# Dilated attention: the score matmuls of two heads issued in turn, in the two row halves of TensorE and two PSUM banks

## The chip, the cores and the metric

The kernel runs on one core of one Trainium2 chip. The metric is the device time of one execution in microseconds; before the change it is 2756.3 us, the median of 3 runs (2753.86 to 2757.47).

In the views of the profile PE is TensorE (its matmuls), PEld its weight loads, DVE is VectorE, ACT is ScalarE, POOL is GpSimd and SP the engine that issues most transfers. L1087 is line 1087 of the kernel.

## What is computed

The reference is a two-layer encoder over 768 tokens, 512 of one sequence and 256 of another. Each layer has a mixer of four branches (a convolution module, spatial gating, latent attention, dilated attention), joined by sigmoid gates, and a convolutional feed-forward part. The change touches one step of the dilated attention. It has three groups (window, dilation) of four heads of 64 dimensions; a group's scores are the products of each query with the keys at multiples of the dilation inside its window:

```
DIL_GROUPS = ((128, 1), (512, 4), (2048, 16))
for g, (win, dil) in enumerate(DIL_GROUPS):
    n_side = (win // 2) // dil
    idx = pos[:, None] + (dil * jnp.arange(-n_side, n_side + 1))[None, :]
    ...
    s = jnp.einsum('bqhd,bqjhd->bhqj', qi[:, :, g], kg, preferred_element_type=jnp.float32)
    s = jnp.where(valid[None, None], s, NEG_INF)
    lse = jax.nn.logsumexp(s, axis=-1)
    p = jnp.exp(s - lse[..., None])
    outs.append(jnp.einsum('bhqj,bqjhd->bqhd', p.astype(vg.dtype), vg))
```

The groups' outputs are then weighted by a softmax over their lse and projected.

## The kernel before

All instructions are unrolled and written out in one order by Python. The large matrices are multiplied as split products: an operand is cut into a high and a low part in the fp32r type, and three matmuls stand for one (`tm`, `fm`; L522 and L498). They are TensorE's main work. Beside them run generators: `go_fast` and `go` put a generator into a list, and `q`, called after each block of split matmuls, moves a planned clock on and lets the generators that are due issue their next instructions. So the small steps of the attention are sprinkled between the matmuls of the projection that runs as the main work. The planned clock sets an order only; on the chip each engine takes its instructions in that order.

For each layer, `mixer` projects dilation group 0, then starts `dil_attn(0)` as a generator and projects group 1, and so on; the attention of group 2 runs beside the projection of the spatial gating. In `dil_proj` the results are normalised and rotated (`dil_norm`), and PE transposes them into `qT` and `kT` (the tile `q`, read by L1029 on ACT and L1030 on DVE). A feature block of 128 partitions, `qT[y]`, holds two heads: head 2y in partitions 0 to 63 and head 2y+1 in 64 to 127. The tokens of groups 1 and 2 are taken with a stride, so there the projection's weight operand is a strided slice of the normalised input.

`dil_attn` makes jobs, two for each block of queries: `par` 0 does the lower heads of both feature blocks, `par` 1 the upper ones. In group 0 a block is one tile of 128 queries with 192 or 256 keys; in groups 1 and 2 it is two tiles with 128 keys each. `pipe` runs the jobs as a pipeline of seven stages: in step i it issues `score` of job i, then `done` of job i-3; a third of a step later `low` of job i and `turn` of job i-1; another third later `expo` of job i, `copy` of job i-1 and `value` of job i-2. The planned step is 2.7 us for group 0 and 4.0 us for the others.

- `score` (L1087, PE): 2 or 4 matmuls of 64 rows in float32, into a PSUM tile `sc` of its own.
- `low` (L1092, L1094, DVE): adds the mask out of `sc` into `P` and takes the minimum of each row.
- `expo` (L1101, ACT): the exponentials.
- `turn` (PE transposes, L511), `copy` (L1121 or L1123, DVE), `value` (L1135 or L1138, PE), `done` (L1144, ACT, and the store to DRAM).

PSUM has eight banks. The mixer's pool keeps two double banks for the projections (`mm`) and four single ones (`ps`), which `sc`, the transposes `pt`, the values `po` and the projection's `q` share. A bank that has been read comes back to the end of the list of free ones.

The score matmuls of one job all lie in the same half of the array's rows: 0 to 63 for `par` 0, 64 to 127 for `par` 1. A job's matmuls stand between split matmuls of 128 rows.

Of the kernel before, what the change touches and what calls it, by code (L numbers as in the profile page):

```python
# [247 lines left out]
class Net:  # L248
# [814 lines left out]
    def dil_job(self, g, si, t0, n, i0, nt, par, qT, kT, v, vs, sh):  # L1063
        nc = self.nc
        if g == 0:
            lo, hi = max(0, 128 * i0 - 64), min(128 * n, 128 * i0 + 192)
            mk = self.h("m0")[:, lo - 128 * i0 + 64:hi - 128 * i0 + 64]
            W = hi - lo
            z = 128 * i0 + 64 - lo
            blocks = ((0, z, vs[si][i0][0:z]), (z, W, vs[si][i0 + 1][0:W - z]))  # L1070
            ts = ((t0 + i0, 128 * t0 + lo),)
        else:
            mk = self.h("m0")[:, 64:192] if (g, si) == (1, 0) else self.h(f"m{g}" + "sp"[si])
            W = 128
            ts = tuple((t, 128 * t) for t in (t0 + i0, t0 + i0 + 1))
        rr = slice(64 * par, 64 * par + 64)
        e = {}

        def score():
            if par == 0:  # L1080
                sh["ot"] = ot = self.pm.tile([128, nt, 264], F32, tag="ot", name=self.nm("ot"), bufs=3)
                sh["ol"] = ot[:, :, 256:260].rearrange("p t (h q) -> p t h q", q=2)
                sh["om"] = ot[:, :, 260:264].rearrange("p t (h q) -> p t h q", q=2)
            e["sc"] = sc = self.ps([128, nt, 2, 256 // nt])
            for x, (t, k0) in enumerate(ts):
                for y in range(2):
                    nc.tensor.matmul(sc[:, x, y, 0:W], qT[y][rr, 128 * t:128 * t + 128], kT[y][rr, k0:k0 + W],  # L1087
                                     start=True, stop=True)

        def low():  # L1090
            e["P"] = P = self.s(nt * 2 * W).rearrange("p (a w) -> p a w", a=nt * 2)
            nc.vector.tensor_add(P, e.pop("sc")[:, :, :, 0:W].rearrange("p t h w -> p (t h) w"),  # L1092
                                 mk.unsqueeze(1).broadcast_to([128, nt * 2, W]))
            nc.vector.tensor_reduce(sh["om"][:, :, :, par], P.rearrange("p (t h) w -> p t h w", t=nt), axis=AX.X,  # L1094
                                    op=ALU.min)

        def expo():
            P = e["P"]
            for x in range(nt):
                for y in range(2):  # L1100
                    nc.scalar.activation(P[:, 2 * x + y, :], P[:, 2 * x + y, :], AF.Exp,  # L1101
                                         bias=sh["om"][:, x, y, par:par + 1], scale=-1.0,
                                         accum_out=sh["ol"][:, x, y, par:par + 1])

        def turn():
            P = e.pop("P")
            e["pt"] = pt = self.ps([128, 4, 128])
            if g == 0:
                for y in range(2):
                    for z, (a, c, _) in enumerate(blocks):  # L1110
                        self.tr(pt[0:c - a, 2 * z + y, :], P[:, y, a:c])
            else:
                for y in range(4):
                    self.tr(pt[:, y, :], P[:, y, :])

        def copy():
            pt = e.pop("pt")
            e["PT"] = PT = self.s().rearrange("p (a q) -> p a q", a=4)
            if W == 192:
                for z, (a, c, _) in enumerate(blocks):  # L1120
                    nc.vector.tensor_copy(PT[0:c - a, 2 * z:2 * z + 2, :], pt[0:c - a, 2 * z:2 * z + 2, :])  # L1121
            else:
                nc.vector.tensor_copy(PT, pt)  # L1123

        def value():
            PT = e.pop("PT")
            if par == 0:
                sh["po"] = self.ps([128, nt, 4, 64])
            po = sh["po"]
            for x, (t, _) in enumerate(ts):  # L1130
                for y in range(2):
                    hc = slice(64 * (2 * y + par), 64 * (2 * y + par) + 64)
                    if g == 0:
                        for z, (a, c, vv) in enumerate(blocks):
                            nc.tensor.matmul(po[:, 0, 2 * y + par, :], PT[0:c - a, 2 * z + y, :], vv[:, hc], start=(z == 0),  # L1135
                                             stop=(z == 1))
                    else:
                        nc.tensor.matmul(po[:, x, 2 * y + par, :], PT[:, 2 * x + y, :], v[t // 3][:, t % 3, hc], start=True,  # L1138
                                         stop=True)

        def done():
            if par == 1:
                ot = sh["ot"]
                nc.scalar.copy(ot[:, :, 0:256].rearrange("p t (h d) -> p t h d", d=64), sh["po"])  # L1144
                self.go_fast(self.dil_store(g, [t for t, _ in ts], ot), 1.0)
                sh.clear()

        return score, low, expo, turn, copy, value, done

    def dil_store(self, g, ts, ot):  # L1150
# [626 lines left out]
```

## Time and profile before

| | |
|---|---|
| median of 3 runs | 2756.3 us |
| the profiled execution, its own time | 2762.6 us |
| its span, first to last instruction | 2760.8 us |
| mean granted TensorE clock | 0.987 |
| TensorE busy (matmuls) | 2709.3 us, 98% |
| weight loads busy | 2461.6 us, 89% |
| VectorE busy | 1731.8 us, 63% |
| ScalarE busy | 1142.6 us, 41% |
| DMA | 258.87 MB, mean 94 GB/s |

Shares are averages over stages with different limits. Matmuls are pipelined and the ends in the rows are modelled, so starts say more than durations; the weight loads run beside the matmuls. The granted clock is given as a share of TensorE's upper level.

### The profile page before, as it was taken

To read this page: it belongs to the slowest core of one execution; us is meant where nothing else is said; L and a number is where in the kernel's file an instruction comes from. 1 tells how busy PE (TensorE), PEld (TensorE's weight loads), DVE (VectorE), ACT (ScalarE), POOL (GpSimd) and SP (SyncE) were. 2 spreads that over 40 slices of the span, in tenths; PEclk is the share of its full clock that TensorE was granted. 3 is DMA by queue.
4 is the path that set the end of the run, shared out by engine and by line. 5 is a ranking of instruction groups with operands and counts; after the bars stand their busy time and mean duration, and the time that the engine had idled before them with its cause. 6 is when DMAs were issued, how large, how long until landed. Compare 5 with 4: busy or idle time off the path is not lost.

```text
span 2760.8 us, 40139 instructions
## 1 busy us (share of the span) xinstructions
PE 2709.3 (98%) x15196; PEld 2461.6 (89%) x15196; DVE 1731.8 (63%) x3048; ACT 1142.6 (41%) x2333; POOL 631.8 (23%) x592
## 2 busy tenths in 40 slices
PE   9999999999999899999999999999999989999999
PEld 8778998888898899999987789888888988999998
DVE  6644347787437966686746443477874378666875
ACT  6443334223224554554544433342232245544553
POOL 3402123112222212222315021221221222122221
PEclk9999999999999999999999999999999999999999
DMA  5101013221233366646721010132212324566566
GB/s 165 43 28 37 30 61 100 71 65 58 62 131 83 95 146 138 148 123 146 190 93 43 28 39 32 58 113 62 62 61 65 127 80 112 144 130 153 130 135 164
DMA packets 143264, 258.87 MB, mean 94 GB/s; under 512 B 20192, under 2 KB 36192, under 8 KB 143072
## 3 DMA queue, kind: packets, MB, share of 16 engines
q1 hardware_dynamic: 118368, 197.59, 22.6%
q0 software_dynamic: 24704, 58.73, 12.3%
q8 instruction: 119, 1.95, 0.3%
q14 instruction: 73, 0.60, 0.1%
HBM read 205.78 MB, written 48.91 MB: 92 GB/s over the span
## 4 chain that ended last, share of the span: by engine, by line
PE 87%; DVE 8%; issue 2%; ACT 2%; POOL 1%; DMA 1%; SPq 0%; DVEq 0%; ACTq 0%; POOLq 0%
PE mm L498 34%; PE ps L498 27%; PE mm L522 16%; PE ps L511 3%; PE ps L1087 2%; DVE wlo L453 2%; PE ps L904 1%; PE ps L1135 1%; PE ps L937 1%; PE ps L1138 1%; POOL st L529 1%; DVE b L612 1%; DVE hl L628 0%; PE ps L851 0%; DMA raw<-wu 0%
## 5 line engine op out<-in xcount | busy, mean ns | idle before, releaser
L453 DVE TENSOR_TENSOR wlo<-raw,whi 128x512 fp32r<-128x512 f32 (+1 forms) x616 | 480.9, 790 | 139.6 <-ACT whi L444 116.3
L498 PE MATMUL ps<-b,whi 128*128 128x384 f32 (+2 forms) x1888 | 466.4, 340 | 17.2 <-ACT s L1530 11.7
L444 ACT CAST whi<-raw 128x512 fp32r<-128x512 f32 (+1 forms) x616 | 370.6, 614 | 243.4 <-PE ps L498 72.2
L498 PEld LDWEIGHTS ps<-b,whi 128*128 128x128 f32 x1888 | 329.9, 191 | 34.3 <-ACT s L1530 12.4
L498 PE MATMUL mm<-b,whi 128*128 128x512 f32 (+1 forms) x1504 | 323.0, 336 | 0.4 <-DVE b L1574 0.4
L522 PE MATMUL mm<-whi,hh 128*128 128x512 f32 (+2 forms) x752 | 312.7, 416 | 7.6 <-ACT hh L547 5.7
L498 PE MATMUL mm<-hh,whi 128*128 128x512 f32 (+1 forms) x1152 | 302.1, 343 | 0.0
L498 PE MATMUL ps<-b,wlo 128*128 128x384 f32 (+2 forms) x944 | 299.6, 339 | 0.0
L498 PE MATMUL mm<-hh,wlo 128*128 128x512 f32 (+1 forms) x1152 | 296.9, 339 | 0.0
L498 PE MATMUL mm<-hl,whi 128*128 128x512 f32 (+1 forms) x1152 | 294.9, 337 | 0.0
L522 PE MATMUL mm<-whi,hl 128*128 128x512 f32 (+2 forms) x752 | 278.6, 371 | 0.8 <-DVE hl L554 0.8
L522 PE MATMUL mm<-wlo,hh 128*128 128x512 f32 (+2 forms) x752 | 278.3, 370 | 0.0
L498 PE MATMUL ps<-hh,whi 128*128 128x384 f32 x768 | 260.3, 339 | 8.5 <-ACT whi L444 8.5
L498 PE MATMUL ps<-hl,whi 128*128 128x384 f32 x768 | 260.0, 338 | 1.2 <-DVE hl L628 1.2
L498 PEld LDWEIGHTS mm<-b,whi 128*128 128x128 f32 x1504 | 237.1, 188 | 26.5 <-DVE b L1574 1.1
L498 PE MATMUL ps<-hh,wlo 128*128 128x384 f32 x768 | 258.7, 337 | 0.0
L529 POOL TENSOR_TENSOR st<-st,mhalf 128x16 f32<-128x16 f32 (+5 forms) x50 | 94.9, 1899 | 601.5 <-DVE st L1012 372.5
L1366 POOL TENSOR_TENSOR b<-b,b 128x768 f32<-128x768 f32 x48 | 100.2, 2087 | 463.4 <-DVE b L1361 406.9
L522 PEld LDWEIGHTS mm<-whi,hh 128*128 128x128 f32 x752 | 177.3, 236 | 29.8 <-issue 13.6
L498 PEld LDWEIGHTS mm<-hh,whi 128*128 128x128 f32 x1152 | 177.4, 189 | 26.5 <-issue 3.3
L498 PEld LDWEIGHTS mm<-hl,whi 128*128 128x128 f32 x1152 | 175.7, 188 | 25.0
L498 PEld LDWEIGHTS mm<-hh,wlo 128*128 128x128 f32 x1152 | 176.1, 188 | 24.2
(233 smaller groups left out, 4658.9 us busy)
## 6 DMA issues: line engine op xcount, KB each, us to landing
raw<-wu SPq DMA_DIRECT2D x600, 256.0 KB, 2.7
xsp<-y POOLq DMA_DIRECT2D x66, 384.0 KB, 6.0
raw<-wu POOLq DMA_DIRECT2D x80, 256.0 KB, 4.9
b<-xsp SPq DMA_DIRECT2D x24, 384.0 KB, 7.2
xsp<-b POOLq DMA_DIRECT2D x22, 384.0 KB, 5.8
do<-ot SPq DMA_DIRECT2D x36, 132.0 KB, 1.8
b<-do SPq DMA_DIRECT2D x12, 384.0 KB, 3.6
raw<-wu SPq DMA_DIRECT2D x16, 208.0 KB, 4.1
```

Source lines behind the costliest of these rows:

```text
L444: self.nc.scalar.copy(hi, raw)
L453: self.nc.vector.tensor_sub(lo, raw, hi.bitcast(F32))
L498: nc.tensor.matmul(ap, w, x[:, c0:c1], start=(k == 0 and i == 0 and not more), stop=(k == K - 1 and i == 2), skip_group_check=more)
L511: self.nc.tensor.transpose(out, x, self.ident)
L522: nc.tensor.matmul(ap, x[:, cols], w, start=(k == 0 and i == 0), stop=(k == 7 and i == 2))
L529: self.nc.gpsimd.tensor_tensor(r, ms, self.mhalf[:, 0:n], op=ALU.pow)
L612: nc.vector.scalar_tensor_tensor(h, h, g[:, k:k + 1], self.rbc[:, cols], op0=ALU.mult, op1=ALU.mult)
L904: nc.tensor.matmul(sc[:, 0:S], qkT[hh][:, 128 * t:128 * t + 128], qkT[4 + hh][:, 128 * t0:128 * t0 + S], start=True, stop=True)
L937: nc.tensor.matmul(sh["po"][:, hh, :], PT[:, 128 * kb:128 * kb + 128], v[(t0 + kb) // 3][:, (t0 + kb) % 3, 64 * hh:64 * hh + 64], start=(k ...
L1087: nc.tensor.matmul(sc[:, x, y, 0:W], qT[y][rr, 128 * t:128 * t + 128], kT[y][rr, k0:k0 + W], start=True, stop=True)
L1135: nc.tensor.matmul(po[:, 0, 2 * y + par, :], PT[0:c - a, 2 * z + y, :], vv[:, hc], start=(z == 0), stop=(z == 1))
L1366: nc.gpsimd.tensor_add(a, a, t)
```

## The change

`score` of the lower heads (`par` 0) now takes two PSUM tiles and issues the matmuls of both jobs of the pair. For each query tile and each feature block it issues the lower head's matmul (rows 0 to 63, first tile) and then the upper head's (rows 64 to 127, second tile). `score` of the upper heads issues nothing and takes its tile out of the shared dictionary `sh`. All other stages are as they were, and so are the planned times.

```diff
@@ dil_job
-        rr = slice(64 * par, 64 * par + 64)
         e = {}
 
         def score():
@@
                 sh["ol"] = ot[:, :, 256:260].rearrange("p t (h q) -> p t h q", q=2)
                 sh["om"] = ot[:, :, 260:264].rearrange("p t (h q) -> p t h q", q=2)
-            e["sc"] = sc = self.ps([128, nt, 2, 256 // nt])
-            for x, (t, k0) in enumerate(ts):
-                for y in range(2):
-                    nc.tensor.matmul(sc[:, x, y, 0:W], qT[y][rr, 128 * t:128 * t + 128], kT[y][rr, k0:k0 + W],
-                                     start=True, stop=True)
+
+                sh["sc"] = [self.ps([128, nt, 2, 256 // nt]) for _ in range(2)]
+                for x, (t, k0) in enumerate(ts):
+                    for y in range(2):
+                        for sc, rr in zip(sh["sc"], (slice(0, 64), slice(64, 128))):
+                            nc.tensor.matmul(sc[:, x, y, 0:W], qT[y][rr, 128 * t:128 * t + 128],
+                                             kT[y][rr, k0:k0 + W], start=True, stop=True)
+            e["sc"] = sh["sc"].pop(0)
```

## Rows read from the trace of the kernel before

**Rows 1.** The page, busy time by engine: us, share of the span, instructions.
```profile
PE 2709.3 (98%) x15196; PEld 2461.6 (89%) x15196; DVE 1731.8 (63%) x3048; ACT 1142.6 (41%) x2333; POOL 631.8 (23%) x592
```

**Rows 2.** The chain that ended last, shares of the span by line.
```profile
PE mm L498 34%; PE ps L498 27%; PE mm L522 16%; PE ps L511 3%; PE ps L1087 2%; DVE wlo L453 2%; PE ps L904 1%; PE ps L1135 1%; PE ps L937 1%; PE ps L1138 1%; POOL st L529 1%; DVE b L612 1%; DVE hl L628 0%; PE ps L851 0%; DMA raw<-wu 0%
```

**Rows 3.** Stretches: length, busy us by engine, then clock, DMA; first and sum.
```profile
207.00:290.00 83.00, 83.00 (x390) 72.62 (x390) 35.95 (x70) 27.25 (x78) 20.31 (x27) 0.96 0.10 32
...
sum 307.00, PE 307.00 PEld 267.75 DVE 129.05 ACT 108.39 POOL 60.73; mean PE 51.17 PEld 44.62 DVE 21.51 ACT 18.07 POOL 10.12
```

**Rows 4.** Line L1087: duration ns min/median/max, starts, forms; who waited (us, times).
```profile
L1087 PEld LDWEIGHTS ps<-b,b x288: 182/188/334, 207.5 to 1796.9; 64*128 64x128 f32 x144
L1087 PE MATMUL ps<-b,b x288: 272/272/686, 207.5 to 1797.0; 64*128 64x128 f32 x96, 64*128 64x192 f32 x32, 64*128 64x256 f32 x16
...
  DVE s L1092: 115.6, 34
```

**Rows 5.** Timeline of PE, group 0: start us, us, engine, line, op, tiles, shapes, count.
```profile
206.73 0.40 PE L522 MATMUL mm<-whi,hh 128*128 128x512 f32 x1
...
207.20 0.40 PE L522 MATMUL mm<-whi,hl 128*128 128x512 f32 x1
207.53 0.92 PE L1087 MATMUL ps<-b,b 64*128 64x192 f32 x4
...
208.83 0.40 PE L522 MATMUL mm<-wlo,hh 128*128 128x512 f32 x1
```

**Rows 6.** Timeline of PE around a score group of dilation group 1.
```profile
339.89 0.40 PE L522 MATMUL mm<-whi,hl 128*128 128x512 f32 x1
340.22 1.16 PE L1087 MATMUL ps<-b,b 64*128 64x128 f32 x8
...
341.64 0.39 PE L522 MATMUL mm<-wlo,hh 128*128 128x512 f32 x1
```

**Rows 7.** Timeline of PE, narrow windows: second and last instruction of both groups.
```profile
207.79 0.48 PE L1087 MATMUL ps<-b,b 64*128 64x192 f32 x2
...
208.12 0.32 PE L1087 MATMUL ps<-b,b 64*128 64x192 f32 x1
...
340.43 0.38 PE L1087 MATMUL ps<-b,b 64*128 64x128 f32 x2
...
341.10 0.27 PE L1087 MATMUL ps<-b,b 64*128 64x128 f32 x1
```

**Rows 8.** Timeline of PE around value matmuls of group 0 and group 1.
```profile
223.33 0.40 PE L522 MATMUL mm<-whi,hl 128*128 128x512 f32 x1
223.66 1.52 PE L1135 MATMUL ps<-b,s 64*128 64x64 f32 x8
...
225.44 0.40 PE L522 MATMUL mm<-wlo,hh 128*128 128x512 f32 x1
...
337.47 0.39 PE L522 MATMUL mm<-whi,hl 128*128 128x512 f32 x1
337.70 1.00 PE L1138 MATMUL ps<-b,s 128*128 128x64 f32 x8
...
338.95 0.40 PE L522 MATMUL mm<-wlo,hh 128*128 128x512 f32 x1
```

**Rows 9.** Timeline of PE, the transposes of the job scored at 207.53.
```profile
215.42 0.60 PE L511 MATMUL ps<-hc,s 128*64 128x128 f32 x4
```

**Rows 10.** Timeline of all engines at the pair scored at 262.74.
```profile
259.90 0.60 PE L511 MATMUL ps<-hc,b 128*128 128x128 f32 x4
...
261.73 0.35 DVE L1030 TENSOR_SCALAR b<-ps,mc 128x128 f32<-128x128 f32 x1 [0.43 <-ACT b L1029]
...
262.47 0.35 ACT L1144 COPY ot<-ps 128x256 f32<-128x256 f32 x1
262.59 0.74 DVE L1121 COPY s<-ps 128x256 f32<-128x256 f32 x2
...
262.74 0.91 PE L1087 MATMUL ps<-b,b 64*128 64x192 f32 x4
```

## The prediction

> **What bounds the kernel now.** I read the page first. TensorE is busy for 98% of the span [rows 1], and the chain that ended last runs through PE for nearly all of it; the score matmuls of this change, L1087, hold 2% of that chain, some 55 us [rows 2]. Busy is no proof of being the bound, so next come the six stretches in which dilated attention runs (three groups, two layers), summed by engine: PE is busy for all 307.00 us of 307.00, while VectorE has 129 and ScalarE 108 [rows 3]. Nothing there makes PE wait. Whatever PE is spared in these stretches, the end should be spared too.
>
> The line's own view shows 288 instructions for 144 matmuls: a float32 matmul is issued as two, each with a weight load of its own [rows 4]. Of the 144, 96 are 128 columns wide, 32 are 192 and 16 are 256. They come in 48 groups (one per job): 4 instructions in dilation group 0, 8 in the others; so 24 pairs of jobs, 12 of either kind (8 pairs at 192 and 4 at 256 columns; 12 at 128).
>
> Then the timeline around one group. Two projection matmuls start 0.47 us apart (206.73, 207.20). From the last projection matmul before the scores (207.20) to the second one after them (208.83) there are 1.63 us; less the two normal steps, the group costs PE 1.16 us [rows 5]. In the same way the 8-instruction group costs 341.64 - 339.89 - 0.47 = 1.28 us [rows 6]. Narrow windows give the pace inside: (208.12 - 207.79)/2 = 0.165 us an instruction at 192 columns, (341.10 - 340.43)/6 = 0.112 at 128 [rows 7]; by the same slope 0.218 at 256 (an estimate from those two). So 4 x 0.165 = 0.66 of the 1.16, and 8 x 0.112 = 0.89 of the 1.28 is streaming; 0.50 and 0.39 us remain as the price of going into half the rows and back. The 0.50 belongs to groups before a projection whose tokens are read with a stride (10 of 24 in a layer), the 0.39 to the other 14.
>
> **The change part by part.** *Half of the entries and exits go.* 24 groups instead of 48. The removed ones are every second job: 4 of a layer's 12 cost 0.50, 8 cost 0.39. 2 x (4 x 0.50 + 8 x 0.39) = 10.2 us off PE. This part needs no overlap at all.
>
> *The order inside a pair.* Heads in rows 0 to 63 and 64 to 127 take turns by matmul, and a matmul being two instructions, PE sees A A B B A A B B. No row of this trace has two row sets at work at once, so the stream is bounded from both sides. Nothing overlaps: 0 us. Everything overlaps that program order lets: A2 waits for A1 (same rows), B1 may run beside A2, A3 beside B2; n instructions then take n/2 + 1 slots where they took n. That is 3 slots less for a pair in group 0, 7 in the others: 8 x 3 x 0.165 + 4 x 3 x 0.218 + 12 x 7 x 0.112 = 4.0 + 2.6 + 9.4 = 16.0 us. With n/2 slots exactly, one slot per pair more: 3.5. In between, weight loads may stay one behind the other: the value matmuls of L1138, only 64 columns wide, hold PE for 338.95 - 337.47 - 0.47 = 1.01 us for 8, no faster than 128 columns do [rows 8], so about 0.112 is a floor that columns don't set. With that floor kept, the 128-wide pairs gain nothing and the others 8 x 8 x (0.165 - 0.112) + 4 x 8 x (0.218 - 0.112) = 3.4 + 3.4 = 6.8 us. I take 16.0: a load takes 188 ns in its row [rows 4] while loads follow each other every 112 ns, so even in the same rows two are in flight at once, and I see no reason for other rows to do worse.
>
> The Trainium skill speaks for that end in "TensorEngine Tiling (Array Packing)", Key Properties: tiles work independently and can load weights and multiply in parallel, and it is a change of the tiling mode, not of the tile, that drains the array. Rows 5 and 6 agree with the second half as far as they go (0.39 to 0.50 us for one change there and back). Against it stands "TensorE: Matmul & The Clock Gate", section LDWEIGHTS: a load takes its columns over 1.2, 107 ns for 128, whatever the rows; if there is one loader, the sum is the floor's, 17.0 us in all instead of 26.2.
>
> *When the scores are ready.* The first head's matmuls now end one slot before the pair's end: 5 slots x 0.165 instead of 4, or 9 x 0.112 instead of 8, some 0.1 to 0.2 us later (without any overlap up to 0.9). The masked add on DVE takes them next, and DVE waits for them already [rows 4]. Behind it come the reduction and the exponentials, and then PE's transposes of the same job: after the scores of 207.53 those start at 215.42 [rows 5, 9], one step later in the pipeline, and PE finds their input ready. 0.9 us fits in. If that cover were gone, PE would wait for it on the path, at most 24 x 0.2 = 5 us. The second head's scores are ready a whole step early; their consumers keep their places. No DMA is issued, removed or moved past a queue; the adds, exponentials and copies are the same instructions.
>
> *Two banks held at once.* There are four single banks here (8 - 2 x 2), for scores, transposes, values and, on and off, the next projection's transposes (the tile q). The second head's bank is now taken one step (5 to 9 us) early. I went through the jobs in program order: score, score, value and q make four at once, and one place in each layer has a fifth, the pair at 262.74. There the value tile is still being copied out by L1144 (262.47, 0.35 us), the transposes by L1121 (262.59, 0.74 us), and the fourth bank comes only when L1030 has read q, 261.73 + 0.35 = 262.08, so 0.66 us before PE wants it [rows 10]. A new wait, but one that has already ended. I take 0. Were it late, everything on PE stands behind it in order, the projection too.
>
> Sum: 10.2 + 16.0 = 26.2 us. The profiled execution took 2762.6 us (span 2760.8), 6.3 above the median of the runs, so its like should come to 2736.4, and the median to 2756.3 - 26.2 = 2730.1.
>
> **Rivals.** *Loads are serial.* The rows work side by side but the 0.112 us floor holds for all loads: 10.2 + 6.8 = 17.0, 2739 us. For it: the 64-column matmuls of rows 8. Against it: loads of 188 ns every 112.
>
> *No overlap at all*, the change doesn't do what it says: only entries and exits are saved, 10.2 us, 2746. For it: nothing in the trace shows two row sets at work.
>
> *Slower: each change of rows stalls the array.* L1135 goes between 64 and 128 rows four times in 8 instructions; it takes 225.44 - 223.33 = 2.11 us where L1138 with its eight takes 1.48 [rows 8], 0.158 us a change. If moving from the lower to the upper half cost the same, A A B B has 3 changes in a group-0 pair and 7 in the others: 12 x 3 + 12 x 7 = 120. 120 x 0.158 = 19.0, less 10.2: 8.8 us slower, 2765; with half of the 0.39 as the price (0.195) 13.2 slower, 2770. It decides from 10.2/120 = 0.085 us a change. Against it: those changes are of how many rows are used, not of which.
>
> *Banks.* If the pair at 262.74 has to wait for the whole read of q (259.90 to 262.08 in the trace, 2.2 us), twice: 4.4 us, 2735. To eat the gain it would need 26.2/24 = 1.1 us at every pair, which ends at 2756; the margin of 0.66 at the tightest place speaks against it.
>
> **Chances.** Full overlap 0.42, serial loads 0.24, none 0.15, stalls 0.13, banks 0.06. The likeliest gives 2730. The range goes from 2725 (n/2 slots, 29.7 us, and the scatter of the runs) to 2748 (no overlap, with scatter): it holds the first three and so 0.81. About 0.2%, 5.5 us, is what a measurement of this kernel can tell from no change. Faster takes the first three, 0.81; the banks go to no change, 0.06; slower is the stalls, 0.13.
>
> **What the profile after would show.** 24 groups of 8 or 16 instructions; entry and exit still 0.4 to 0.5 us for each. Full overlap: a 16-instruction group takes about 9 x 0.112 + 0.39 = 1.4 us of PE beyond the two normal steps where two took 2.56; starts of A2 and B1 almost together. Serial loads: starts 0.112 apart at all widths, 16 in 2.2 us. None: 0.165 at 192 columns as before. Stalls: gaps of 0.1 us or more before each third instruction. Banks: PE idle before a score or a q, released by DVE or ACT. The prediction is wrong if PE starts to wait in these stretches, or if the time comes back after them: the clock was at 0.96 over the first stretch [rows 3], so 0.04 x 83 = 3.3 us is what the low clock can have cost there, and a different beat of the array may shift that by as much either way.

## The result, and the profile after

| | before | after |
|---|---|---|
| median | 2756.9 us (4 runs) | 2728.5 us (4 runs, 2727.0 to 2730.1) |
| ratio | 1 | 0.9888, 95% interval 0.9876 to 0.9900 |
| span of the profiled execution | 2760.8 us | 2728.4 us |
| mean granted TensorE clock | 0.987 | 0.989 |

The kernel is 28.4 us faster (1.1%); forecast were 26.2 us and 2730. On another chip the same kernel came to 2727.8 us, ratio 0.9885 (0.9870 to 0.9900).

The page after, busy time by engine and the chain that ended last, answers to [rows 1, 2]:

```profile
PE 2677.2 (98%) x15196; PEld 2439.2 (89%) x15196; DVE 1729.2 (63%) x3048; ACT 1141.3 (42%) x2333; POOL 634.0 (23%) x592
...
PE mm L498 35%; PE ps L498 26%; PE mm L522 16%; PE ps L511 3%; DVE wlo L453 2%; PE ps L904 1%; PE ps L1137 1%; PE ps L937 1%; PE ps L1088 1%; DMA raw<-wu 1%; PE ps L1140 1%; POOL st L529 1%; DVE b L612 1%; DVE hl L628 0%; PE ps L851 0%
```

The instructions are as many as before. PE is busy for 32.1 us less and still for 98% of the span; the scores, now L1088, have gone from 2% of the chain to 1%. PE stays without a pause where the attention runs. The table of stretches again, its sum alone; the six stretches end where the last scores of a dilation group are issued, which is one job earlier now, so the 240 us are not to be compared with the 307 of [rows 3], only PE's 240.00 with the length:

```profile
sum 240.00, PE 240.00 PEld 214.75 DVE 118.88 ACT 93.55 POOL 57.82; mean PE 40.00 PEld 35.79 DVE 19.81 ACT 15.59 POOL 9.64
```

The timeline of PE around a score pair of group 0, and around one of group 2, answers to [rows 5, 6]:

```profile
207.77 0.40 PE L522 MATMUL mm<-whi,hl 128*128 128x512 f32 x1
208.10 0.92 PE L1088 MATMUL ps<-b,b 64*128 64x192 f32 x8
...
209.41 0.40 PE L522 MATMUL mm<-wlo,hh 128*128 128x512 f32 x1
...
376.14 0.39 PE L522 MATMUL mm<-whi,hl 128*128 128x512 f32 x1
376.46 1.16 PE L1088 MATMUL ps<-b,b 64*128 64x128 f32 x16
...
377.89 0.39 PE L522 MATMUL mm<-wlo,hh 128*128 128x512 f32 x1
```

The pair of eight instructions costs PE 209.41 - 207.77 - 0.47 = 1.17 us, where one job of four cost 1.16 [rows 5]. Sixteen cost 377.89 - 376.14 - 0.47 = 1.28 us, as eight did [rows 6]. A pair costs what one of its jobs did: the second head is free. Summed in this way over the whole trace, 48 groups took 61.5 us before and 24 take 31.2 after: 30.3 of the 32.4 us between the two spans. Three of the 48 and one of the 24 ran at the lower clock, in whole or in part, which, set beside their likes, cost some 1.5 and 0.8 us; at one clock the groups give 29.6. The other 2.1 I have not followed to a line. The clock was at its lower level a little less (0.989 for 0.987), and the two profiled executions are not equally typical: the one before took 5.7 us more than its median, the one after 1.7.

Narrow windows show the starts (a row gives the first start and how many matmuls are in flight):

```profile
208.10 0.43 PE L1088 MATMUL ps<-b,b 64*128 64x192 f32 x2
...
208.10 0.60 PE L1088 MATMUL ps<-b,b 64*128 64x192 f32 x4
```

The first of these windows is 208.11 to 208.12, the second 208.50 to 208.52. Two score matmuls have started within 0.02 us of each other; at 208.5, when one half of the rows alone would have its second under way, there are four.

### The profile page after: what moved, and what is told of

Read it like the earlier page. It is cut to its first block, busy times and chain, and to the rows that moved or that the text cites. A ratio compares the mean times of both kernels' runs of the same rounds, so it can differ in the third digit from the quotient of the medians.

```text
span 2728.4 us, 40139 instructions
## 1 busy us (share of the span) xinstructions
PE 2677.2 (98%) x15196; PEld 2439.2 (89%) x15196; DVE 1729.2 (63%) x3048; ACT 1141.3 (42%) x2333; POOL 634.0 (23%) x592
## 4 chain that ended last, share of the span: by engine, by line
PE 86%; DVE 8%; issue 2%; ACT 2%; POOL 1%; DMA 1%; SPq 0%; DVEq 0%; ACTq 0%; POOLq 0%
PE mm L498 35%; PE ps L498 26%; PE mm L522 16%; PE ps L511 3%; DVE wlo L453 2%; PE ps L904 1%; PE ps L1137 1%; PE ps L937 1%; PE ps L1088 1%; DMA raw<-wu 1%; PE ps L1140 1%; POOL st L529 1%; DVE b L612 1%; DVE hl L628 0%; PE ps L851 0%
## 5 line engine op out<-in xcount | busy, mean ns | idle before, releaser
L522 PEld LDWEIGHTS mm<-whi,hh 128*128 128x128 f32 x752 | 177.6, 236 | 25.6 <-issue 10.2
```

The source lines that it names most:

```text
L522: nc.tensor.matmul(ap, x[:, cols], w, start=(k == 0 and i == 0), stop=(k == 7 and i == 2))
```

## The experiments

All are compared with the kernel before on the same chip. The edits are shown against the kernel after the change, where nothing else is said; `...` marks lines left out.

**One head after the other.** The pair in one group and two banks, without the turns:

```diff
-                for x, (t, k0) in enumerate(ts):
-                    for y in range(2):
-                        for sc, rr in zip(sh["sc"], (slice(0, 64), slice(64, 128))):
+                for sc, rr in zip(sh["sc"], (slice(0, 64), slice(64, 128))):
+                    for x, (t, k0) in enumerate(ts):
+                        for y in range(2):
```

> The pair's matmuls in one group and two banks as after the change, but all of the lower head first, then all of the upper head. Theory A (each row half takes its own instructions as they come; order inside the group does not matter): as after the change, about 2728 us, and starts of both halves together in the trace. Rival B (strict program order, alternation is needed; only the last lower and first upper matmul can meet): 24 entries saved, 10.2 us, and one slot a pair, 3.5 us: about 2743. Rival C (the halves never overlap, the gain is elsewhere): 10.2 us, 2746.

Measured: 2734.7 us, ratio 0.9908 (0.9895 to 0.9922). Neither A nor B nor C: by the ratios 0.0020 x 2757 = 5.5 us behind the change, and 11.6 us ahead of strict order, whose 13.7 us would be a ratio of 0.9950. The timeline of PE, a pair of group 0 and one of group 2:

```profile
207.05 0.40 PE L522 MATMUL mm<-whi,hl 128*128 128x512 f32 x1
207.38 0.93 PE L1088 MATMUL ps<-b,b 64*128 64x192 f32 x8
...
208.70 0.40 PE L522 MATMUL mm<-wlo,hh 128*128 128x512 f32 x1
...
378.30 0.39 PE L522 MATMUL mm<-whi,hl 128*128 128x512 f32 x1
378.61 1.71 PE L1088 MATMUL ps<-b,b 64*128 64x128 f32 x16
...
380.59 0.39 PE L522 MATMUL mm<-wlo,hh 128*128 128x512 f32 x1
```

With four instructions of the lower head ahead of the upper head's, the pair takes 208.70 - 207.05 - 0.47 = 1.18 us: full overlap in spite of the order. With eight ahead it takes 380.59 - 378.30 - 0.47 = 1.82, 0.54 more than after the change. Two windows on the first pair of group 1, at 299.60 and at 299.64, show where the second head comes in:

```profile
299.40 0.38 PE L1088 MATMUL ps<-b,b 64*128 64x128 f32 x2
...
299.40 0.60 PE L1088 MATMUL ps<-b,b 64*128 64x128 f32 x4
```

The group starts at 299.07. Up to 299.60 matmuls follow each other at one half's pace (two in flight); in between two start together, the lower head's fifth and the upper head's first. So three of the lower head (the sixth to the eighth) were waiting and were passed by. In group 0, with four in all, three wait behind the first: the same number. 0.54 x 12 pairs = 6.5 us, which is the distance to the change: summed over the trace the groups take 37.8 us here and 31.2 there.

**In turns of two matmuls.** That reach, tried by itself:

```diff
                 for x, (t, k0) in enumerate(ts):
-                    for y in range(2):
-                        for sc, rr in zip(sh["sc"], (slice(0, 64), slice(64, 128))):
+                    for sc, rr in zip(sh["sc"], (slice(0, 64), slice(64, 128))):
+                        for y in range(2):
```

> As after the change, but the heads change over after every two matmuls (four instructions) instead of after each: A A A A B B B B, and in groups 1 and 2 the same once more. In the run with one head after the other, the upper head's first instruction started beside the lower head's first where four instructions stood ahead of it, and only beside the fifth where eight stood ahead: three may wait ahead of it. If that is a reach of the queue, this order overlaps fully: groups as long as after the change, a ratio of 0.989. If each change-over costs, or only one slot of each change-over overlaps, 16-instruction groups take 0.3 us or more longer than after, and the ratio is 0.990 or above.

Measured: 2727.4 us, ratio 0.9878 (0.9861 to 0.9894), like the change; a group of sixteen is 0.1 us longer than after (378.37 - 376.52 - 0.47 = 1.38):

```profile
376.52 0.39 PE L522 MATMUL mm<-whi,hl 128*128 128x512 f32 x1
376.84 1.26 PE L1088 MATMUL ps<-b,b 64*128 64x128 f32 x16
...
378.37 0.39 PE L522 MATMUL mm<-wlo,hh 128*128 128x512 f32 x1
```

A turn after each matmul isn't needed: four instructions of one head at a time overlap but for that 0.1 us, eight do not.

**Both heads in the same half of the rows.** It leaves out the upper heads' own scores:

```diff
-                        for sc, rr in zip(sh["sc"], (slice(0, 64), slice(64, 128))):
+                        for sc, rr in zip(sh["sc"], 2 * (slice(0, 64),)):
```

> As after the change (pairs in one group, in turn, two banks), but both heads' matmuls read partitions 0 to 63; the upper heads get the lower heads' scores. So entries and exits are halved and nothing can overlap. By the sum: 10.2 us faster than before, a ratio of 0.9963, and groups of 8 x 0.165 or 16 x 0.112 plus 0.4 to 0.5 us. If it were as fast as after the change, the overlap would not be the cause of the rest; if as slow as before, entries and exits would cost nothing.

Measured: 2748.6 us, ratio 0.9963 (0.9949 to 0.9976), 10.6 us below its before, where 10.2 were expected. A plain pair of group 0 at 192 columns:

```profile
248.46 0.40 PE L522 MATMUL mm<-whi,hl 128*128 128x512 f32 x1
248.78 1.56 PE L1088 MATMUL ps<-b,b 64*128 64x192 f32 x8
...
250.63 0.39 PE L522 MATMUL mm<-wlo,hh 128*128 128x512 f32 x1
```

250.63 - 248.46 - 0.47 = 1.70 us: 8 x 0.165 = 1.32 and one entry and exit of 0.38. Order, banks and the number of groups are those of the change, only the second set of rows is missing, and with it go 21 of the 31 us that the change had on the same chip.

**The scores twice,** after the change and before it, so that the stream is doubled and the number of entries stays (the kernel before has the same line, and gets the same edit):

```diff
-                for x, (t, k0) in enumerate(ts):
+                for x, (t, k0) in 2 * tuple(enumerate(ts)):
```

> The kernel after the change with every score matmul issued twice, the second over the first. What it adds is the pure stream of the scores in this form, without entry and exit. If the halves run side by side throughout, 8 x 4 x 0.165 + 4 x 4 x 0.218 + 12 x 8 x 0.112 = 19.5 us more than after the change, about 2748. If they take turns, 39 us more, about 2767.

> The kernel before with every score matmul issued twice. Adds the stream of one row half at a time: 32 x 2 x 0.165 + 16 x 2 x 0.218 + 96 x 2 x 0.112 = 39 us, so 2757 + 39 = 2796 by every theory that has PE as the bound here. If it adds clearly less, the scores were partly hidden and the prices of entry and stream are mis-split.

Measured: after, twice: 2746.8 us, ratio 0.9953 (0.9941 to 0.9966). Against the change's 0.9888 that is 0.0065 x 2757 = 18 us of added stream (19.5 expected); by the timelines the groups take 49.8 us instead of 31.2, 18.6 more, or 19.4 without the 0.8 us that the lower clock cost one group after the change. Before, twice: 2803.7 us, ratio 1.0157 (1.0144 to 1.0171), 43.7 us more, where 39 were expected; in its trace the groups take 104.5 us instead of 61.5, 43.0 more. Part of that is the clock: four of its 48 groups ran while the granted clock was at 0.50, its 1.2 GHz level (before, three lay there, in whole or in part). The stretch ahead of one of them, the group itself, and the clock of the stretch that it fills:

```profile
265.00:285.20 20.20, 20.20 (x105) 18.92 (x104) 8.15 (x19) 5.56 (x20) 6.28 (x9) 1.00 0.03 10
...
284.97 0.40 PE L522 MATMUL mm<-whi,hl 128*128 128x256 f32 x1
285.30 2.92 PE L1087 MATMUL ps<-b,b 64*128 64x192 f32 x8
...
288.56 0.44 PE L522 MATMUL mm<-wlo,hh 128*128 128x256 f32 x1
...
285.30:288.20 2.90, 2.90 (x10) 2.46 (x9) 0.00 (x0) 0.00 (x0) 0.00 (x0) 0.50 0.04 15
```

It costs 288.56 - 284.97 - 0.47 = 3.12 us, where eight such instructions in one half took 1.70 above; four of these are 5.7 us too many. PE was busy for all 20.20 us before that fall, at a clock of 1.00. What the excess of the median comes from stays open all the same. The profiled execution, with these four groups in it, took 2798.9 us, only 38.9 above the median before. The other three took 2802.0 to 2806.3, each at a mean clock of 0.985 where the executions before had 0.987 to 0.989; that fits more time at the lower level, but of them there is no trace.

**The upper head in half matmuls,** to tell the two heads apart by their shapes:

```diff
-                        for sc, rr in zip(sh["sc"], (slice(0, 64), slice(64, 128))):
-                            nc.tensor.matmul(sc[:, x, y, 0:W], qT[y][rr, 128 * t:128 * t + 128],
-                                             kT[y][rr, k0:k0 + W], start=True, stop=True)
+                        for sc, rr, n in zip(sh["sc"], (slice(0, 64), slice(64, 128)), (1, 2)):
+                            for c in range(0, W, W // n):
+                                nc.tensor.matmul(sc[:, x, y, c:c + W // n], qT[y][rr, 128 * t:128 * t + 128],
+                                                 kT[y][rr, k0 + c:k0 + c + W // n], start=True, stop=True)
```

> As after the change, but each matmul of the upper head is split into two of half the columns, so that the two heads can be told apart in the trace. Theory A (own order in each half): the first instructions of both heads start together, the lower head keeps its pace, the upper head takes 8 x 0.112 = 0.90 us in 192- and 256-column pairs and 16 x 0.112 = 1.79 us in the others: 8 x 0.24 + 4 x 0.02 + 12 x 0.90 = 13 us more than after, about 2741. Rival B (strict program order): the upper head's first instruction starts a slot after the lower head's second, and the group is longer still, about 2745 or more.

Measured: 2741.3 us, ratio 0.9931 (0.9918 to 0.9945): 0.0043 x 2757 = 12 us behind the change, 13 expected by theory A. The time alone would not part the theories (2741 and 2745, with an interval of some 3.7 us to either side); the trace does. Groups of instructions by shape in the window 208.50 to 208.53, at the beginning of a group, and two rows of the window 208.50 to 209.60, nearly the whole group (count, busy us, mean ns):

```profile
L1089 PE MATMUL ps<-b,b 64*128 64x192 f32 x1 | 0.4, 427 | 0.0
L522 PE MATMUL mm<-whi,hl 128*128 128x512 f32 x1 | 0.4, 396 | 0.0
L1089 PE MATMUL ps<-b,b 64*128 64x96 f32 x1 | 0.3, 347 | 0.0
...
L1089 PE MATMUL ps<-b,b 64*128 64x96 f32 x8 | 1.1, 281 | 0.0
L1089 PE MATMUL ps<-b,b 64*128 64x192 f32 x4 | 0.9, 349 | 0.0
```

One instruction of 192 columns (lower head) and one of 96 (upper head) are in flight: the first of the one and the first of the other, though the lower head's matmul is two instructions and both stand ahead. In the whole group the eight narrow ones fill 1.1 us and the four wide ones 0.9 us of the same stretch. Theory A holds here, B falls. In the pairs of groups 1 and 2 the reach shows again, with the heads in each other's place: four instructions of the upper head stand between two and two of the lower head's, and though only 64 columns wide they start 0.112 us apart, as the lower head's do. In the first such pair (from 299.73) the lower head's seventh instruction starts 0.95 us after its first, where its own pace would have it start after 0.77: at the moment when only three that stand ahead of it are still waiting.

**Group 0 alone.** In groups 1 and 2 each job issues its own scores, as before:

```diff
-                sh["sc"] = [self.ps([128, nt, 2, 256 // nt]) for _ in range(2)]
+                sh["sc"] = [self.ps([128, nt, 2, 256 // nt])]
+                if g == 0:
+                    sh["sc"].append(self.ps([128, nt, 2, 256 // nt]))
+                    for x, (t, k0) in enumerate(ts):
+                        for y in range(2):
+                            for sc, rr in zip(sh["sc"], (slice(0, 64), slice(64, 128))):
...
+            if g:
+                if par:
+                    sh["sc"] = [self.ps([128, nt, 2, 256 // nt])]
+                rr = slice(64 * par, 64 * par + 64)
                 for x, (t, k0) in enumerate(ts):
                     for y in range(2):
...
+                        nc.tensor.matmul(sh["sc"][0][:, x, y, 0:W], qT[y][rr, 128 * t:128 * t + 128],
+                                         kT[y][rr, k0:k0 + W], start=True, stop=True)
```

> The change in dilation group 0 alone; groups 1 and 2 issue as before. By the sum with n/2 slots: entries and exits 2 x (2 x 0.50 + 4 x 0.39) = 5.1 us, stream 8 x 4 x 0.165 + 4 x 4 x 0.218 = 8.8 us: 13.9 us faster than before, ratio 0.995. If the banks or the clock matter, the parts do not add up to the whole.

Measured: 2744.3 us, ratio 0.9946 (0.9931 to 0.9960), 14.9 us; 13.9 were expected. That leaves 16.4 of the 31.3 us on this chip for groups 1 and 2, where the sum has 15.8. They were not run alone; within the interval, some 4 us to either side, the parts add up.

**The value matmuls in another order.** The prediction's price for a change between 64 and 128 rows [rows 8], put to use on top of the change:

```diff
-                        for z, (a, c, vv) in enumerate(blocks):
-                            nc.tensor.matmul(po[:, 0, 2 * y + par, :], PT[0:c - a, 2 * z + y, :], vv[:, hc], start=(z == 0),
-                                             stop=(z == 1))
+                        order = sorted(enumerate(blocks), key=lambda b: (b[1][1] - b[1][0]) * (1 - 2 * y), reverse=True)
+                        for k, (z, (a, c, vv)) in enumerate(order):
+                            nc.tensor.matmul(po[:, 0, 2 * y + par, :], PT[0:c - a, 2 * z + y, :], vv[:, hc], start=(k == 0),
+                                             stop=(k == 1))
```

> After the change, and in the value matmuls of dilation group 0 the 128-row block goes first for the first feature block and the 64-row block first for the second, so that the two 64-row blocks stand side by side: 2 changes between 64 and 128 rows instead of 4, in 16 jobs. By the price of rows 8 (0.158 us a change) 16 x 2 x 0.158 = 5.1 us less than after the change, ratio to before about 0.987. If a change of rows costs nothing outside the score groups, the same time as after.

Measured: 2721.4 us, ratio 0.9859 (0.9843 to 0.9876), 6.4 us less than the change's 2727.8 on the same chip, the fastest version here. The first value group in its trace:

```profile
219.71 0.39 PE L522 MATMUL mm<-whi,hl 128*128 128x512 f32 x1
219.94 1.28 PE L1138 MATMUL ps<-b,s 128*128 128x64 f32 x8
...
221.47 0.40 PE L522 MATMUL mm<-wlo,hh 128*128 128x512 f32 x1
```

221.47 - 219.71 = 1.76 us, where the same group took 2.11 [rows 8]: two changes of rows fewer, 0.35 us. Summed in the same way over the 16 groups it is 30.6 us after the change on the same chip and 25.6 here: 5.0 of the 6.4 us, where 5.1 were expected. The other 1.4 were not followed.

**The change once more.**

> The kernel after the change once more, beside the others on the same chip: a ratio of 0.989 again.

Measured: 2727.8 us, ratio 0.9885 (0.9870 to 0.9900).

Heads in different rows but in one bank, which would show whether the second bank is needed, were not tried; that stays open.

## Why the prediction was right, point by point

- *PE bounds these stretches.* Right: what PE was spared (30.3 us by the groups) came off the end (28.4 and 31.3 us in two comparisons), and PE did not begin to wait in these stretches.
- *Half of the entries and exits, 10.2 us.* Right, and shown alone: 10.6 us with both heads in the same rows. The reason given for the two prices is only half right. Five of the 14 groups at 0.39 (255.70 to 288.06 in the trace before) also stand before strided tokens, but before matmuls of 256 columns, and where the clock is full they cost 0.38 (271.56 - 270.05 - 0.47 - 0.66); the 0.50 is seen only where strided tokens and 512 columns come together. The count, and so the sum, is not touched by it.
- *Overlap of the stream, 16.0 us.* The kind was right, the size too small by one slot a pair, 3.5 us. The step that failed is "everything overlaps that program order lets": order does not hold the upper head back, and n instructions take n/2 slots, not n/2 + 1. In the trace two matmuls start together from the first on; the experiments with other orders show that up to three waiting matmuls of the other half are passed by. n/2 slots make 19.5 us and 29.7 in all, the lower end of the range; measured were 28.4 and 31.3.
- *Loads of both halves side by side.* Right: at 128 columns each half keeps its 0.112 us, and both together do 16 instructions in the time of 8. The serial floor, the strongest rival, is out, and so is one loader for both halves. The Trainium skill, "TensorEngine Tiling (Array Packing)", Key Properties, agrees with the trace: tiles load and multiply at once, and a change of tile within the mode costs nothing that shows in these 1.28 us.
- *No overlap* and *a stall at each change of rows* were the other rivals. The first is what the run in the same rows looks like (2749); the second would need gaps before every third instruction, and the groups have no room for any. The price it was taken from is real (two fewer changes between 64 and 128 rows saved 0.35 us), but a change from one half to the other does not pay it.
- *Scores ready a little later for the first head.* Right as far as it shows: PE waits for none of these transposes.
- *The bank at the tightest pair.* The bank is free in time, as forecast, but that pair is not the tightest. Timeline after the change around it, and ahead of it around the fourth pair of the layer, which the prediction passed over:

```profile
244.15 0.68 DVE L1094 TENSOR_TENSOR s<-ps,hc 128x512 f32<-128x512 f32 x1
...
244.87 0.69 DVE L1096 TENSOR_REDUCE ot<-s 128x2 f32<-128x512 f32 x1
...
245.59 0.40 PE L522 MATMUL mm<-whi,hl 128*128 128x512 f32 x1
...
245.92 0.63 PEld L1088 LDWEIGHTS ps<-b,b 64*128 64x128 f32 x8 [0.36 <-DVE ot L1096]
245.92 0.92 PE L1088 MATMUL ps<-b,b 64*128 64x192 f32 x8
...
257.43 0.35 DVE L1030 TENSOR_SCALAR b<-ps,mc 128x128 f32<-128x128 f32 x1 [0.44 <-ACT b L1029]
...
258.17 0.35 ACT L1146 COPY ot<-ps 128x256 f32<-128x256 f32 x1
...
258.43 0.63 PEld L1088 LDWEIGHTS ps<-b,b 64*128 64x128 f32 x8
258.43 0.92 PE L1088 MATMUL ps<-b,b 64*128 64x192 f32 x8
```

  At the forecast pair the fourth bank is read out at 257.78, 0.65 us before the scores want it (0.66 in [rows 10]), and the scores start 0.32 us after the last projection matmul (258.11), as elsewhere. At the other pair the profile has the score loads wait for DVE's L1096, presumably for the bank that L1094 just before it reads. L1096 ends at 245.56, 0.36 us ahead of the scores, and they start 0.33 us after the last projection matmul (245.59): nothing is lost, but the margin is about half of the one forecast.

## What to carry to other kernels

Matmuls that use half of the array's rows are worth pairing with others that use the other half, in banks of their own: the second set was free here, weight loads included, and here the turns had to be only so fine that no more than three of one half's matmuls wait ahead of the other's. Whether one bank for both would do was not tried. Apart from any overlap, each excursion from 128 rows to 64 and back cost 0.4 to 0.5 us beyond its stream, so gather such instructions, and order what stands between so that the row count changes seldom. To price it, take the start of the second matmul after a group less the last one before it, less two normal steps: that holds entry, stream and exit, which the busy time does not.

## What was not expected of the hardware

A matmul of one half starts ahead of matmuls of the other half that stand before it in the program: three were passed, in different orders, and with eight ahead the second half sat idle until the fifth had begun. So the sentence ahead of the prediction that each engine takes its instructions in the written order does not hold for these matmuls. And within that reach the two halves keep separate paces: with the upper head in matmuls of 96 columns, both began together and each went on at its own. What sets the reach at three is not shown.
